# A transformer layer's out and gate products on one core: a fourth place for raw weight pieces

## The chip, the cores and the metric

The kernel runs on one core of one Trainium2 chip. A core has five engines that run side by side, each with its own queue of instructions: TensorE (PE in the profile; its weight loads are listed apart as PEld), VectorE (DVE), ScalarE (ACT), GpSimd (POOL) and SyncE (SP, which here only starts transfers). Transfers between the chip's memory (HBM) and the core's on-chip memory (SBUF) are made by 16 DMA engines. Matrix products land in a second small memory (PSUM), whose banks hold 128 x 512 numbers.

The metric is the device time of one execution in microseconds, the median of several runs. The kernel before takes 797.68 us (three runs, 797.63 to 797.83).

## The reference, cut to what matters

One layer: sliding-window attention over 512 tokens of width 2048, an output product, and a gated embedding. All in float32.

```python
hn = rmsnorm(x, norm_g[0])
y = swa_mixer(hn, ...)               # (attention(hn) * silu(gate)) @ w_out
x = x + y
emb = p[0] @ ple_proj[0]             # 512 x 256 @ 256 x 2048
g = sigmoid(rmsnorm(x, ple_norm[0]) @ ple_gate[0])
x = x + emb * g
return rmsnorm(x, final_g)
```

Two large weighted stages stand behind the attention: the product with `w_out` (2048 x 2048) and the product with `ple_gate` (2048 x 2048).

## The kernel before, in words

**Precision.** TensorE's fast 32-bit format keeps fewer bits than float32. So every operand is split into a high part, rounded to that format, and a low part, the rest; a product is made of three matmuls, high x high, low x high and high x low. The helper `mm3` issues them (lines 128 to 130 of the profile). For a raw weight piece, ScalarE makes the high part (`bhi`, line 675) and VectorE then the low one (`blo`, line 676). This pair is called the split of the piece here.

**Stages.** First the keys, values and first queries; then the remaining projections, with attention woven in (until about 450 us); then the out stage (`w_out`) and the gate stage (`ple_gate`), each computed by Strassen's scheme: seven products of half-size matrices instead of eight, in the order `ORDER_OUT` = 1, 7, 2, 6, 5, 3, 4 and `ORDER_PLE` = 2, 7, 1, 6, 5, 3, 4. The last product of the gate stage ends the kernel, together with the last normalisation and the stores.

**Units and pieces.** A unit is one product p for one half jj of the columns. It takes four pieces of weights of 128 x 1024 numbers (512 KB); each piece serves 12 matmuls of 128 x 512 (two halves, two blocks of tokens, three terms). In the gate stage some units are followed by a piece of `ple_proj` and its 12 matmuls (`e` in the profile; those of the gate are `g`, of the out stage `o`). The pieces of both stages are numbered through, 0 to 111, by the class `Pieces`. Three kinds exist: `one` and `proj` are loaded into a place for raw pieces (tile names `braw`); `seed` and `grow` pieces live in tiles of their own (`grown`), where later weights are added in by GpSimd's transfers.

**Places for raw pieces.** The pool `wpool` has three buffers of the tag `wraw`. `_prepare(n)` takes the next one and has SP start the load (line 668). SP starts the transfers in program order, and each waits until its buffer's previous piece is split. `ahead(i)`, called when TensorE comes to piece i, prepares pieces up to i + 3 and splits up to i + 2; the high and low tiles have three buffers each.

**Sums of the weights and of the left side.** The left operands (`Forms.steps`) are made from the gated attention output (`gate0` to `gate3`): some products need a difference first (VectorE, line 768, 128 x 1024 in place), then the split into `fho` (ScalarE, line 780) and `flo` (VectorE, line 781). Lines 585, 595 and 601 finish the gated output itself.

**What sets the order.** TensorE's and SP's order is the order of the program text everywhere. During the attention all engines' order is written out by hand. From the end of the attention to the first product of the gate stage the order on ScalarE, VectorE and GpSimd is chosen by the framework's scheduler when the program is built, from its own estimate of when operands and buffers come free; from the second product of the gate stage on (`manual_schedule` with all five engines) it is by hand again. Each engine carries out its instructions strictly in that order.

**Pools.** The attention's tiles live in pools that are closed at its end; the pool `late` (in the list `rooms`) takes over their space. A tile of `late` waits for the last user of the bytes under it.

Of the kernel before, what the change touches and what calls it, by code (L numbers as in the profile page):

```python
# [11 lines left out]
F32 = mybir.dt.float32  # L12
# [8 lines left out]
P = 128  # L21
KC = D // P
NB = S // P
# [15 lines left out]
MASKED = -3.0e38  # L39
TOEP = 384  # L40
WARM = 24
PAD = 48
XW = S + 1 + 768


# [11 lines left out]
def trunk_kernel(ctx: ExitStack, tc: tile.TileContext, a: dict):  # L57
    nc = tc.nc

    def pool(name, bufs=1, **kw):  # L60
        return ctx.enter_context(tc.tile_pool(name=name, bufs=bufs, **kw))
# [3 lines left out]
    const = pool("const")  # L65
# [2 lines left out]
    banks_s = ExitStack()  # L68
    others = {"s": banks_s.enter_context(tc.tile_pool(name="psum_s", bufs=2, space=PSUM))}

    const.tile([P, PAD], F32, name="pad")
    pn = const.tile([P, KC], F32, name="pn")

    whole = pool("whole", bufs=4)
    wpool = pool("wpool", bufs=3)
# [12 lines left out]
    WE = 1024  # L88

    class Weights:  # L90


        def __init__(self, ahead):
            self.srcs, self.ahead, self.raw, self.made = [], ahead, [], []

            self.todo, self.asked, self.apart = [], 0, False
# [37 lines left out]
    ident = const.tile([P, P], F32, name="ident")  # L134
    make_identity(nc, ident)

    warm = const.tile([P, 1], F32, name="warm")
    nc.vector.memset(warm, 1.0)
    nc.scalar.activation(warm, warm, AF.Sqrt)
    ones = nc.const_aps.tensor(1.0, [P, P], mybir.dt.bfloat16)  # L140
# [14 lines left out]
    v_ps = [bank(f"vps{t}", "ttoo"[t]) for t in range(NB)]  # L155

    rstd1 = const.tile([P, NB], F32, name="rstd1")
    ssq1 = const.tile([P, NB], F32, name="ssq1")

    def run(gen):  # L160
        for _ in gen:
# [2 lines left out]
    def rsqrt_mean(out, ssq, n, nm):  # L164

        w = out.shape[-1]
        ms = const.tile([P, w], F32, name=f"ms_{nm}")
        rt = const.tile([P, w], F32, name=f"rt_{nm}")
        y = const.tile([P, w], F32, name=f"y_{nm}")
        t = const.tile([P, w], F32, name=f"t_{nm}")  # L170
        nc.vector.tensor_scalar(ms, ssq, 1.0 / n, EPS, op0=ALU.mult, op1=ALU.add)
        nc.scalar.activation(rt, ms, AF.Sqrt)
        yield
        nc.vector.reciprocal(y, rt)
        nc.vector.tensor_mul(t, y, y)
        nc.vector.tensor_mul(t, t, ms)
        nc.vector.tensor_scalar(t, t, -0.5, 1.5, op0=ALU.mult, op1=ALU.add)
        nc.vector.tensor_mul(out, y, t)
# [21 lines left out]
    for k in range(KC):  # L200
# [57 lines left out]
        f, e = k == 0, k == KC - 1  # L258
# [26 lines left out]
        if 3 <= k < 3 + NB:  # L285
            t = k - 3
# [3 lines left out]
        if k == 9:  # L290
            run(rsqrt_mean(rstd1, ssq1, D, "r1"))

            rdram = tc.dram_tile([NB, P], F32, name="rdram")
            nc.gpsimd.dma_start(rdram.rearrange("t p -> p t"), rstd1)
            nc.gpsimd.dma_start(rb, rdram.rearrange("t p -> (t p)").partition_broadcast(P))
# [91 lines left out]
    for b in range(exact, BUCKETS):  # L387
        d = np.nonzero(bk == b)[0]
        if len(d):
            lo, n = P - 1 + int(d.min()), len(d)  # L390
# [229 lines left out]
    rooms = []  # L620
# [7 lines left out]
    def block(nm, r, c, jj, m):  # L628
        return a[nm][2 * (c - 1) + jj, 4 * (r - 1) + m]

    SUMS = [("w_out", 7), ("w_out", 5), ("w_out", 6), ("ple_gate", 7), ("ple_gate", 5)]
    for nm, p in SUMS:
        for jj in range(2):
            for m in range(4):
                t = summed[nm, p, jj, m] = tc.dram_tile([P, WE], F32, name=f"{nm}_{p}_{jj}_{m}")
# [12 lines left out]
    class Pieces:  # L648
# [9 lines left out]
        def _prepare(self, i):  # L658
            kind, src, key = self.specs[i]
            if kind == "grow":  # L660
                t = self.grown[key]
                nc.gpsimd.dma_start(t, src, accum_op=ALU.add)
            else:
                if kind == "seed":
                    t = self.grown[key] = rooms[0].tile([P, WE], F32, tag="grown", name=f"grown{i}", bufs=8)
                else:
                    t = wpool.tile([P, WE], F32, tag="wraw", name=f"braw{i}")
                nc.sync.dma_start(t.rearrange("p (k c) -> p k c", k=2) if kind == "proj" else t, src)
            self.base[i] = t

# [13 lines left out]
            nc.vector.tensor_sub(lo, raw, hi.bitcast(F32))  # L684
            self.made[i] = tuple([t[:, :512], t[:, 512:]] for t in (hi, lo))

        done = 0

        def ahead(self, i):

            last = len(self.specs) - 9
            for n in range(max(i, 0), min(i + 6, last) + 1):
                kind = self.specs[n][0]
                if n not in self.base and n >= self.done and kind != "grow" and (kind == "seed" or n <= i + 3):
                    self._prepare(n)
            while self.done <= min(i + 2, last):
                self._split(self.done)
                self.done += 1
# [298 lines left out]


    rstd2 = const.tile([P, NB], F32, name="rstd2")
    ss2 = const.tile([P, NB], F32, name="ss2")  # L1000
    pT = wpool.tile([P, WE], F32, tag="wraw", name="pT").rearrange("p (k t) -> p k t", k=2)
    nc.sync.dma_start(pT, a["pT"])
    nc.scalar.copy(pTh, pT)
# [1 line left out]
    done = {t: 0 for t in range(NB)}  # L1005
# [81 lines left out]
    for n, p in enumerate(ORDER_PLE[:-1]):  # L1087
# [8 lines left out]
        for jj in range(2):  # L1096
            calls = iter(range(4))

            def todo():
                k = early.get((p, jj, next(calls)))  # L1100
                if turns:
                    turn(*turns.pop(0), "s")
                    if not turns:
                        nc.vector.tensor_reduce(ss2, ssq2, axis=AX.X, op=ALU.add)
                        run(rsqrt_mean(rstd2, ss2, D, "r2"))
                    return
                next(nxt, None)
                if p == 2:
                    next(nxt, None)
                if k is not None:  # L1110
                    split_last(k)

            ps = unit(p, jj, at_ple, ple_forms, todo)
            e = {}
            if p in (1, 5, 3):
                w = B.get(at_ple[p, jj] + 4)
                for t in (0, 1) if p in (1, 3) else (2, 3):
                    e[t] = embed(t, w, "to"[jj])
            if (p, jj) != (3, 1):
                later.insert(0, partial_of(gate_later, p, jj, ps, e))  # L1120
# [5 lines left out]
    w = [B.get(at_ple["e", jj]) for jj in range(2)]  # L1126
    f = ple_forms.made[4]
# [27 lines left out]
    ssum = const.tile([P, 3], F32, name="ssum")  # L1155
    nc.vector.tensor_reduce(ssum[:, :2], ssq3[:, :2, :4], axis=AX.X, op=ALU.add)
    root = rsqrt_mean(yn2[:, :2], ssum[:, :2], D, "r3")
    next(root)
    g = block(0, 0, "s", "o")()
# [30 lines left out]
    next(g)  # L1190
    run(g)

    base, ms, rt, im, ys, nw, yn = (const.tile([P, 1], F32, name=f"{v}_3") for v in ("base", "ms", "rt", "im", "ys", "nw", "yn"))
    g = block(1, 1, "p", "t", slice(0, 256))()
    next(g)
    by_gain(3, 0)
# [2 lines left out]
    n = done[3]  # L1199
# [87 lines left out]
```

## Time and profile before

| what | value |
|---|---|
| median of the runs | 797.68 us |
| the profiled execution | 799.05 us, of which the span (first to last instruction) 797.0 us |
| TensorE busy | 786.0 us, 99% of the span |
| VectorE busy | 589.4 us, 74% |
| ScalarE busy | 500.1 us, 63% |
| mean granted TensorE clock | 0.996 |
| splits of raw pieces, VectorE | 80 of 1.22 us each |
| matmuls 128 x 512 in the two stages | 0.39 us each, overlapped |

How to read the rows in this document: a row of the timeline has start, length, engine, line, operation, result<-operands, shape and count; in square brackets the idle time before it and what ended it. A row merges neighbours ("x2") and its length then covers both. Matmul rows overlap, since the next begins before the last is out of the array; the steps between starts count. In the chain of work that ended last, a row is start, length, engine, result and line. SPq rows are the moments at which SP starts a transfer; how long the transfer takes isn't in their length. A row of a table by stretches gives the stretch, its length, busy time and instructions of PE, PEld, DVE, ACT and POOL, then the granted clock, the DMA engines' share and GB/s.

### The profile page before, as it was taken

The page shows a single profiled execution, that of the slowest core. Times are in us where ns is not written, and L with a number is a line of the kernel's source. Part 1 is how long each engine was busy: PE and PEld are TensorE (multiplying, and loading weights), DVE is VectorE, ACT ScalarE, POOL GpSimd, SP SyncE. Part 2 cuts the span into 40 slices and gives each one's busy share as a digit, 9 for nine tenths or more (in the row PEclk, how much of TensorE's full clock was granted, in tenths as well). Part 3 has the DMA queues.
Part 4 walks back from the last instruction along what each step waited for, and adds up shares of the span by engine and source line. Part 5 has one row for each costly group of instructions (what it writes and reads, how often), then busy time and mean ns, then how long its engine had stood idle before and what let it go on. Part 6 is the DMA issues. An engine that isn't in the chain of part 4 may idle for free.

```text
span 797.0 us, 10975 instructions
## 1 busy us (share of the span) xinstructions
PE 786.0 (99%) x3758; PEld 657.5 (82%) x3758; DVE 589.4 (74%) x1030; ACT 500.1 (63%) x1057; POOL 115.3 (14%) x234
## 2 busy tenths in 40 slices
PE   9999999999999999999999999999999999999995
PEld 8888888888888888888888888888888888878884
DVE  4546697877878597777768898766656656979996
ACT  5742576675766676676756644555568656646855
POOL 0031223131212213131312100020000120200000
PEclk9999999999999999999999999999999999999998
DMA  9882489697878868677865378997503995775533
GB/s 346 282 221 96 119 259 247 164 252 187 221 186 241 225 180 230 191 234 162 260 161 145 120 276 308 371 248 242 190 28 127 360 219 192 157 204 196 183 106 106
DMA packets 42343, 164.23 MB, mean 206 GB/s; under 512 B 5984, under 2 KB 7008, under 8 KB 38448
## 3 DMA queue, kind: packets, MB, share of 16 engines
q1 hardware_dynamic: 35456, 129.67, 47.7%
q0 software_dynamic: 6832, 33.88, 23.0%
q8 instruction: 29, 0.48, 0.3%
q14 instruction: 26, 0.21, 0.1%
HBM read 157.70 MB, written 46.19 MB: 256 GB/s over the span
## 4 chain that ended last, share of the span: by engine, by line
PE 95%; DVE 2%; DMA 1%; ACT 0%; issue 0%; ACTq 0%; DVEq 0%
PE gps L128 7%; PE gps L130 7%; PE gps L129 7%; PE qps L128 7%; PE qps L130 7%; PE qps L129 7%; PE o L128 6%; PE o L130 6%; PE o L129 6%; PE g L129 5%; PE g L130 4%; PE g L128 4%; PE s L463 2%; PE o L558 2%; PE vps L280 2%; PE pt L516 2%
## 5 line engine op out<-in xcount | busy, mean ns | idle before, releaser
L676 DVE TENSOR_TENSOR blo<-braw,bhi 128x1024 fp32r<-128x1024 f32 x80 | 97.5, 1221 | 40.3 <-ACT bhi L675 40.1
L675 ACT CAST bhi<-braw 128x1024 fp32r<-128x1024 f32 x80 | 84.0, 1051 | 64.9 <-PE o L130 22.7
L128 PE MATMUL gps<-xh,whi 128*128 128x512 f32 x256 | 99.9, 390 | 0.1
L130 PE MATMUL gps<-xh,wlo 128*128 128x512 f32 x256 | 99.8, 390 | 0.0
L129 PE MATMUL gps<-xl,whi 128*128 128x512 f32 x256 | 99.8, 390 | 0.0
L128 PE MATMUL o<-bhi,fho 128*128 128x512 f32 x224 | 87.7, 391 | 0.0
L128 PE MATMUL qps<-xh,whi 128*128 128x512 f32 x224 | 87.7, 391 | 0.0
L130 PE MATMUL qps<-xh,wlo 128*128 128x512 f32 x224 | 87.4, 390 | 0.0
L129 PE MATMUL qps<-xl,whi 128*128 128x512 f32 x224 | 87.3, 390 | 0.0
L129 PE MATMUL o<-blo,fho 128*128 128x512 f32 x224 | 87.2, 389 | 0.0
L130 PE MATMUL o<-bhi,flo 128*128 128x512 f32 x224 | 87.2, 389 | 0.0
L129 PE MATMUL g<-blo,fhg 128*128 128x512 f32 x192 | 75.1, 391 | 0.6 <-DVE blo L676 0.6
L128 PE MATMUL g<-bhi,fhg 128*128 128x512 f32 x192 | 75.1, 391 | 0.0
L112 DVE TENSOR_TENSOR wlo<-wraw,whi 128x1024 fp32r<-128x1024 f32 x60 | 73.8, 1231 | 1.7 <-ACT whi L111 1.3
L130 PE MATMUL g<-bhi,flg 128*128 128x512 f32 x192 | 74.8, 390 | 0.0
L532 POOL TENSOR_SCALAR_AFFINE_SELECT own<-r 64x512 fp32r<-64x512 f32 (+1 forms) x48 | 32.4, 675 | 254.8 <-DVE r L522 254.8
L521 ACT CAST r<-pt 128x256 fp32r<-128x256 f32 x64 | 23.8, 371 | 71.8 <-PE pt L516 71.5
L522 DVE TENSOR_TENSOR r<-pt,r 128x256 fp32r<-128x256 f32 x64 | 27.1, 423 | 55.7 <-ACT r L521 54.9
L111 ACT CAST whi<-wraw 128x1024 fp32r<-128x1024 f32 x60 | 62.3, 1040 | 4.4 <-issue 3.9
L676 DVE TENSOR_TENSOR blo<-grown,bhi 128x1024 fp32r<-128x1024 f32 x32 | 39.1, 1223 | 23.6 <-ACT bhi L675 21.9
L130 PEld LDWEIGHTS gps<-xh,wlo 128*128 128x128 f32 x256 | 48.1, 188 | 10.1
L128 PEld LDWEIGHTS gps<-xh,whi 128*128 128x128 f32 x256 | 48.1, 188 | 9.4 <-PE vps L280 0.5
(206 smaller groups left out, 1738.8 us busy)
## 6 DMA issues: line engine op xcount, KB each, us to landing
wraw<-in_w_gate_in SPq DMA_DIRECT2D x32, 512.0 KB, 5.9
wraw<-in_w_q SPq DMA_DIRECT2D x28, 512.0 KB, 5.0
w_out<-in_w_out POOLq DMA_DIRECT2D x24, 512.0 KB, 7.7
braw<-in_w_out SPq DMA_DIRECT2D x24, 512.0 KB, 4.3
braw<-in_ple_gate SPq DMA_DIRECT2D x24, 512.0 KB, 4.5
xw<-in_first SPq DMA_DIRECT2D x14, 640.5 KB, 6.6
w_out<-in_w_out SPq DMA_DIRECT2D x16, 512.0 KB, 6.2
ple_gate<-in_ple_gate SPq DMA_DIRECT2D x16, 512.0 KB, 6.6
```

What stands on the lines that cost most here:

```text
L111: nc.scalar.copy(hi, raw)
L112: nc.vector.tensor_sub(lo, raw, hi.bitcast(F32))
L128: nc.tensor.matmul(ps, sh, mh, start=first, stop=False, skip_group_check=more)
L129: nc.tensor.matmul(ps, sh, ml, start=False, stop=False, skip_group_check=more)
L130: nc.tensor.matmul(ps, sl, mh, start=False, stop=last, skip_group_check=more)
L280: nc.tensor.matmul(v_ps[t], h[:, c], both[:, :, 256:512], start=f, stop=e, skip_group_check=True)
L463: nc.tensor.matmul(s_ps[:, u, : 2 * n], st, key[:, :, first : first + n], start=True, stop=True)
L521: nc.scalar.copy(rh, src)
L522: nc.vector.tensor_sub(rl, src, rh.bitcast(F32))
L532: nc.gpsimd.affine_select(out=flat(own), in_=flat(r).bitcast(F32), pattern=[[0, 8], [sign, HB]], compare_op=ALU.is_ge, fill=0.0, base=-HB ...
L675: nc.scalar.copy(hi, raw)
L676: nc.vector.tensor_sub(lo, raw, hi.bitcast(F32))
```

## The change

In the two weighted stages a fourth place for raw pieces is added: a tile of the tag `fourth` in the pool `late`. Every fourth raw piece goes there; the others go round the three old buffers. Pieces are asked for four ahead instead of three (once `late` exists, so from piece 3 on). `late` has to be 4096 bytes per partition larger. Room is made among the small tiles: a pad of 48 numbers is dropped, the work columns of the reciprocal roots (`ms`, `rt`, `y`, `t`) share tags, and so do `ssq1` with `ss2` and `warm` with `im_3`.

```diff
-    const.tile([P, PAD], F32, name="pad")
-    warm = const.tile([P, 1], F32, name="warm")
+    warm = const.tile([P, 1], F32, tag="one", name="warm")
-    ssq1 = const.tile([P, NB], F32, name="ssq1")
+    ssq1 = const.tile([P, NB], F32, tag="sums", name="ssq1")
...
     def rsqrt_mean(out, ssq, n, nm):
         w = out.shape[-1]
-        ms = const.tile([P, w], F32, name=f"ms_{nm}")
-        rt = const.tile([P, w], F32, name=f"rt_{nm}")
-        y = const.tile([P, w], F32, name=f"y_{nm}")
-        t = const.tile([P, w], F32, name=f"t_{nm}")
+        of = nm if w == 1 else "r"
+        ms, rt, y, t = (
+            const.tile([P, 1 if w == 1 else NB], F32, tag=f"{v}_{of}", name=f"{v}_{nm}")[:, :w]
+            for v in ("ms", "rt", "y", "t")
+        )
...
     def _prepare(self, i):
...
-                    t = wpool.tile([P, WE], F32, tag="wraw", name=f"braw{i}")
+                    self.raws += 1
+                    if rooms and self.raws % 4 == 0:
+                        t = rooms[0].tile([P, WE], F32, tag="fourth", name=f"braw{i}")
+                    else:
+                        t = wpool.tile([P, WE], F32, tag="wraw", name=f"braw{i}")
...
-        done = 0
+        done = raws = 0
...
     def ahead(self, i):
...
-                if n not in self.base and n >= self.done and kind != "grow" and (kind == "seed" or n <= i + 3):
+                if n not in self.base and n >= self.done and kind != "grow" and (kind == "seed" or n <= i + (4 if rooms else 3)):
                     self._prepare(n)
...
-    ss2 = const.tile([P, NB], F32, name="ss2")
+    ss2 = const.tile([P, NB], F32, tag="sums", name="ss2")
...
-    base, ms, rt, im, ys, nw, yn = (const.tile([P, 1], F32, name=f"{v}_3") for v in ("base", "ms", "rt", "im", "ys", "nw", "yn"))
+    base, ms, rt, ys, nw, yn = (const.tile([P, 1], F32, name=f"{v}_3") for v in ("base", "ms", "rt", "ys", "nw", "yn"))
+    im = const.tile([P, 1], F32, tag="one", name="im_3")
```

The built programs have the same instructions on every engine. The order is the same on TensorE, ScalarE and GpSimd. It differs on SP by the loads that are asked for a piece earlier, and on VectorE in two stretches of the out stage, around pieces 3 to 8 and around pieces 17 and 18. Lines of the changed kernel are numbered four higher than before in the two stages.

More of the change, by code (lines that the diff above doesn't have):

```diff
@@ L41 @@
 WARM = 24
-PAD = 48
 XW = S + 1 + 768
```

## The prediction

> **What bounds the kernel.** I read the page's busy times first, then the chain that ended last, then TensorE's rows wherever that chain leaves TensorE. TensorE (PE) is busy 99% of the span and carries 95% of the chain, so only its gaps are worth anything.
>
> ```profile
> span 797.0 us, 10975 instructions
> PE 786.0 (99%) x3758; PEld 657.5 (82%) x3758; DVE 589.4 (74%) x1030; ACT 500.1 (63%) x1057; POOL 115.3 (14%) x234
> PE 95%; DVE 2%; DMA 1%; ACT 0%; issue 0%; ACTq 0%; DVEq 0%
> ```
>
> In the two weighted stages the chain leaves PE at one place before the tail, through a transfer (start, length):
>
> ```profile
> 700.38 1.23 DVE blo L676
> 701.62 9.11 DMA braw<-ple_gate
> 710.83 1.06 ACT bhi L675
> 711.91 1.24 DVE blo L676
> 713.20 0.50 PE g L129
> 746.13 0.48 PE g L129
> 749.12 0.36 PE g L129
> ```
>
> That is piece 93. All three places were full until the split of piece 90 ended at 701.62; its load then took 9.11 us. TensorE's own rows price this and the two later entries:
>
> ```profile
> 712.19 0.39 PE L128 MATMUL g<-bhi,fhg 128*128 128x512 f32 x1
> 713.20 0.50 PE L129 MATMUL g<-blo,fhg 128*128 128x512 f32 x1 [0.61 <-DVE blo L676]
> 715.82 0.39 PE L128 MATMUL e<-bhi,pTh 128*128 128x512 f32 x1
> 743.02 0.39 PE L128 MATMUL e<-bhi,pTh 128*128 128x512 f32 x1
> 751.61 0.39 PE L128 MATMUL g<-bhi,fhg 128*128 128x512 f32 x1
> ```
>
> Matmuls of this shape start 0.2267 us apart: 715.82 to 743.02 is 27.20 us for 120 of them (ten pieces of twelve: two halves, two token blocks, three products). From 712.19 to 715.82 are 12 starts, due 2.72 us, taken 3.63: **0.91 us lost**. Of this 0.78 is the gap (713.20 against 712.42) and 0.13 a slow restart. From 743.02 to 751.61 are 36 starts, due 8.16, taken 8.59: **0.43 lost**. So the stages have 1.34 us of stall.
>
> **The change, part by part.** *Shared columns, the pad removed.* No instruction is added or removed on any engine; a shared column's earlier readers are done long before it is written again. Zero. Without that cover one such write would wait for one reader, an instruction of this length, in the tail:
>
> ```profile
> 789.43 0.16 DVE L1213 RECIPROCAL im<-ms 128x1 f32<-128x1 f32 x1
> ```
>
> *A fourth place.* Before, the load of piece n waits for the split of n-3, now for that of n-4. Pieces 93 and 103 show what this moves, with the issues of the transfers and the casts:
>
> ```profile
> 678.09 0.32 SPq L668 DMA_DIRECT2D braw<-ple_gate  x1
> 701.62 0.32 SPq L668 DMA_DIRECT2D braw<-ple_gate  x1
> 726.57 0.33 SPq L668 DMA_DIRECT2D braw<-in_ple_gate  x1
> 731.49 0.33 SPq L668 DMA_DIRECT2D braw<-in_ple_gate  x1
> 736.66 1.05 ACT L675 CAST bhi<-braw 128x1024 fp32r<-128x1024 f32 x1 [2.70 <-DVE flg L781]
> 737.74 1.23 DVE L676 TENSOR_TENSOR blo<-braw,bhi 128x1024 fp32r<-128x1024 f32 x1 [1.08 <-ACT bhi L675]
> ```
>
> Piece 92 was issued at 678.09, its place just free; 93 can follow it within some 4 us instead of at 701.62, and 94 takes the slot of 701.62. Even with the same 9.11 us, 94 lands at 710.73 and is split by 713.0, and TensorE first wants it at 715.82 (the e row). So 0.91 goes; next late is nothing nearer than 2.8 us. Piece 103 was issued at 731.49 and cast only at 736.66, 5.17 later; the flg the row names cannot release a cast of weights, so I read a landing. The issue moves to the slot of 726.57, the cast no longer waits, and VectorE (DVE) gets back the 1.08 us it stood idle, more than 105 and 106 were late by. So 0.43 goes too. Gain 1.34 us. Bytes and transfers are unchanged.
>
> *The first use of the fourth place.* Its bytes lie under the last pair's queries, so the first load (piece 3) waits for TensorE's last scores:
>
> ```profile
> 437.85 5.54 SPq L668 DMA_DIRECT2D braw<-in_w_out  x2
> L463 PE MATMUL s<-k,q x4: 312/312/313, 428.7 to 434.5; 128*128 128x320 f32 x4
> ```
>
> These end at 434.8, before piece 2 is issued at 437.85; piece 3, the second of that row (443.07), moves up to 438. Behind it on SP stand only later pieces. Zero.
>
> *What the scheduler does with it.* DVE's order in the out stage is not written out by hand, and the built order differs. TensorE's, ScalarE's and GpSimd's do not. DVE, after the last gate values:
>
> ```
> before: blo3, flo7_10, blo4, flo7_11, gate0-=, blo5, gate1-=, gate0-=, blo6
> after:  flo7_10, flo7_11, gate0-=, gate1-=, gate0-=, blo3, gate1-=, blo4, blo5, blo6
> ```
>
> Five instructions (two of L781, three of L768) now stand ahead of the low half of piece 3, which TensorE needs soon. DVE's rows there before, with the ScalarE (ACT) casts and TensorE's rows that they meet:
>
> ```profile
> 456.60 1.28 DVE L585 SCALAR_TENSOR_TENSOR gate<-gate,u 128x512 f32<-128x512 f32 x2
> 457.80 1.22 DVE L676 TENSOR_TENSOR blo<-braw,bhi 128x1024 fp32r<-128x1024 f32 x1
> 458.94 0.68 DVE L781 TENSOR_TENSOR flo<-gate,fho 128x512 fp32r<-128x512 f32 x1
> 459.54 1.22 DVE L676 TENSOR_TENSOR blo<-braw,bhi 128x1024 fp32r<-128x1024 f32 x1
> 461.27 1.22 DVE L768 TENSOR_TENSOR gate<-gate,gate 128x1024 f32<-128x1024 f32 x1
> 462.41 1.22 DVE L676 TENSOR_TENSOR blo<-braw,bhi 128x1024 fp32r<-128x1024 f32 x1
> 455.17 0.62 ACT L780 CAST fho<-gate 128x512 fp32r<-128x512 f32 x1
> 455.69 1.05 ACT L675 CAST bhi<-braw 128x1024 fp32r<-128x1024 f32 x1
> 451.90 0.40 PE L128 MATMUL o<-bhi,fho 128*128 128x512 f32 x1
> 460.31 0.39 PE L129 MATMUL o<-blo,fho 128*128 128x512 f32 x1
> 497.31 1.22 DVE L676 TENSOR_TENSOR blo<-braw,bhi 128x1024 fp32r<-128x1024 f32 x1
> 450.00:460.00 10.00, 10.00 (x47) 8.34 (x46) 9.96 (x14) 6.99 (x11) 0.04 (x1) 1.00 0.31 107
> ```
>
> DVE is full there (9.96 of 10 us, the windows row), so nothing hides in a hole. All inputs of the five are ready: their last cast ends at 455.79, the gate values before 457.9. Back to back, an L781 takes a step of 0.60 (458.94 to 459.54) and an L768 1.14 (461.27 to 462.41). So blo3 starts at 457.80 + 2 x 0.60 + 3 x 1.14 = 462.42 and ends 1.22 later, at 463.64. Before, it ended at 459.02, 1.29 us ahead of the matmul at 460.31 (the 38th of the stage). That matmul now starts 0.05 after 463.64, as at 713.20 after 713.15: at 463.69, **3.38 us late**, and with the slow restart 0.13 the loss is 3.51. Taking full lengths rather than steps (0.68 and 1.22) gives 463.64 + 0.40 and 3.91: the upper end; the lower, if DVE's start were as much as 0.3 earlier through earlier landings, 3.2.
>
> It ends there: blo4 follows after one more L768 at 464.68 and ends at 465.90, and TensorE reaches it 2.72 after 463.82, at 466.54; blo5 is steps ahead of its need. TensorE is the bound, so nothing gives the time back; what follows is released by TensorE and shifts with it. The order differs once more, where three adds (0.6 each) pass ahead of piece 18: it was split at 497.31 and is due at 451.90 + 18 x 2.72 + 0.23 = 501.09, so 1.8 us do not reach it.
>
> **Sum:** 3.51 - 0.91 - 0.43 = +2.17 us. The profiled execution took 799.05 us (span 797.0 and 2.05 around it), the median of the runs is 797.68; the stalls are the same kind of steps in both, so I add the sum to the median: **799.85 us**, +0.27%. About 0.2% (1.6 us) is what a measurement of this kernel can tell from no change.
>
> **Weighed against a rule.** The granted clock at the end of the span (last column but two):
>
> ```profile
> 786.00:788.00 2.00, 1.52 (x13) 1.32 (x12) 1.79 (x8) 0.68 (x2) 0.00 (x0) 1.00 0.02 8
> 788.00:790.00 2.00, 0.00 (x0) 0.00 (x0) 1.71 (x8) 1.71 (x3) 0.00 (x0) 1.00 0.00 0
> 790.00:792.00 2.00, 0.00 (x0) 0.00 (x0) 1.51 (x4) 1.41 (x3) 0.00 (x0) 0.56 0.20 76
> ```
>
> TensorE stops at 787.52; the clock is whole to 790 and 0.56 on average to 792, so it halves near 790.24, 2.7 us later. The new gap, from the end of the matmul a step before 460.31 (460.08 and 0.39) to 463.69, is 3.2 us. The gap of 0.61 us at 713 halved nothing. The Trainium skill, TensorE: Matmul & The Clock Gate, "Part 1", says the clock halves after an idle window of about 3.4 us, windows running free of the kernel; by it 3.2 us of idle fill no window, and my sum would stand; the trace, which halves after 2.7, does not quite agree.
>
> **Rivals.** (1) *The clock halves in the new gap.* For: 3.2 is over 2.7. Against: at the end the idle followed a nearly empty piece, and it depends on where the gap falls. If it falls about when TensorE resumes, it costs half of the time until it is granted again; 2.7 us as the one delay that I have gives 1.35: 801.2; twice that, 802.5. (2) *Faster: no stall at 460.* It ends on the other side if blo3 is done by 460.26, that is, if the five (4.62 us of steps) fit in holes of DVE before 457.80; then 797.68 - 1.34 = 796.34. The 9.96 of 10 speaks against. (3) *It does not do what it says:* early loads collide with the adds in memory, landing grows with the number under way, and both stalls stay: 797.68 + 3.51 = 801.2. Against: bytes do not grow. (4) *Part-way:* the five overlap better and the stall is 2.9 or less: within 0.2%.
>
> **How the numbers follow.** The sum as it stands 0.56, the clock 0.24, the loads 0.06, part-way 0.08, faster 0.06. The likeliest gives 799.85, with its own range 799.4 to 800.4. For 8 in 10 I reach up to the clock's 801.6 and down to 799.2. Slower by over 0.2%: 0.86; within: 0.08; faster: 0.06.
>
> **What would show it.** In the profile after: a gap of 3.2 us before a matmul on blo near 460.4, released by DVE's blo; ahead of it three L768 (there under a later line) in a row; all DMA issues of the stage one piece earlier; no gap near 716 and 749; the granted clock 1.00 from 460 to 470. I am wrong if blo3 is split before 460, if a new gap stands where the waits of SP were, or if the clock falls in that stretch.

## The result and the profile after

| | before | after |
|---|---|---|
| median of five runs | 797.73 us (797.63 to 798.29) | 803.04 us (802.47 to 803.70) |
| the profiled execution | 799.05 us, span 797.0 | 803.04 us, span 801.0 |

The changed kernel is slower: the ratio is 1.0063, with a 95% interval of 1.0052 to 1.0075. That is 5.31 us between the medians, where +2.17 was forecast; 803.04 lies above the range. The profiled execution of after happens to be its median; that of before is 1.37 us above its own (799.05 against 797.68 of the forecast), which will matter below.

TensorE's rows around 460 us, from the timeline of the kernel after (start, length, engine, line, operation; in brackets the idle time before and what ended it):

```profile
460.36 0.39 PE L128 MATMUL o<-bhi,flo 128*128 128x512 f32 x1
460.59 0.39 PE L126 MATMUL o<-bhi,fho 128*128 128x512 f32 x1
464.19 0.67 PE L127 MATMUL o<-blo,fho 128*128 128x512 f32 x1 [3.22 <-DVE blo L680]
464.66 0.63 PE L128 MATMUL o<-bhi,flo 128*128 128x512 f32 x1
465.08 0.63 PE L126 MATMUL o<-bhi,fho 128*128 128x512 f32 x1
467.22 0.63 PE L128 MATMUL o<-bhi,flo 128*128 128x512 f32 x1
467.64 0.46 PE L126 MATMUL o<-bhi,fho 128*128 128x512 f32 x1
467.94 0.40 PE L127 MATMUL o<-blo,fho 128*128 128x512 f32 x1
468.18 0.39 PE L128 MATMUL o<-bhi,flo 128*128 128x512 f32 x1
```

The step from 460.59 is 3.60 us where 0.2267 is due: 3.37 us late. Then, instead of 0.23, the steps are 0.43 (464.66 to 465.08) until 467.64. From 460.59 to 467.94 are ten steps, due 2.27, taken 7.35: 5.08 us lost in one place. VectorE's rows there:

```profile
456.50 0.69 DVE L594 SCALAR_TENSOR_TENSOR gate<-gps,gate 128x512 f32<-128x512 f32 x1
457.11 1.28 DVE L584 SCALAR_TENSOR_TENSOR gate<-gate,u 128x512 f32<-128x512 f32 x2
458.31 1.29 DVE L785 TENSOR_TENSOR flo<-gate,fho 128x512 fp32r<-128x512 f32 x2
459.51 3.49 DVE L772 TENSOR_TENSOR gate<-gate,gate 128x1024 f32<-128x1024 f32 x3
462.92 1.22 DVE L680 TENSOR_TENSOR blo<-braw,bhi 128x1024 fp32r<-128x1024 f32 x1
```

Two L785 and three L772 stand ahead of the low half of piece 3 (L680 at 462.92, done at 464.14). Its cast was done long before, and its load as well:

```profile
456.20 1.04 ACT L679 CAST bhi<-braw 128x1024 fp32r<-128x1024 f32 x1
```

So VectorE had the operands at 457.24 and was merely ordered to do something else first. What the stall did to the clock is in the table by stretches (stretch, its length, busy time and instructions of PE, PEld, DVE, ACT, POOL, granted clock, DMA share, GB/s). The stretches are cut where the trace's clock records change, at 464.36 and 467.78, and the same length earlier and later:

```profile
457.54:460.95 3.41, 3.41 (x16) 2.50 (x14) 3.41 (x6) 1.22 (x2) 0.00 (x0) 1.00 0.21 84
460.95:464.36 3.41, 0.19 (x2) 0.17 (x2) 3.41 (x4) 0.88 (x1) 0.00 (x0) 1.00 0.00 0
464.36:467.78 3.42, 3.42 (x9) 2.68 (x10) 3.18 (x3) 0.00 (x0) 0.00 (x0) 0.50 0.52 180
467.78:471.19 3.41, 3.41 (x17) 2.79 (x16) 1.23 (x1) 1.12 (x2) 0.00 (x0) 1.00 0.91 280
```

After a stretch in which TensorE was busy 0.19 us, it runs at half clock for exactly one stretch. What that costs follows from the rows: from 464.66 to 467.64 are seven steps, 2.98 us where 1.59 is due, and at that rate a whole stretch of 3.41 us loses 1.6 (less than half of it, since the step at whole clock, 0.227 us, is more than half of the 0.426 at half clock). 3.37 and 1.6 are 4.97; the 0.11 left of 5.08 is about the slow restart that the prediction put at 0.13.

Later in the two stages nothing is left of the waits of before. TensorE's waits of the whole execution, and two stretches that answer to the places of the old stalls, which lie some 4 us later here:

```profile
PE o L127 <- DVE blo L680: 3.2, 1, 3.2
710.00:718.00 8.00, 8.00 (x37) 6.64 (x36) 6.87 (x8) 4.16 (x5) 0.00 (x0) 1.00 0.92 290
745.00:754.00 9.00, 9.00 (x41) 7.46 (x40) 8.93 (x11) 7.44 (x11) 0.00 (x0) 1.00 0.53 150
```

Between the two traces, counted by TensorE's starts, the offset is +0.50 already at 460.36 (the start-up, which differs from execution to execution), 5.59 behind the slow stretch, then 0.89 less at 713 and 0.43 less at 749. So against that one execution the gain is there. Between the medians of five runs it does not show: 5.08 of the 5.31 is the place at 460. But 41 later runs of before, beside the experiments below, have a median of 798.31; 803.04 is 4.73 above that, and then a gain of some 0.35 us would stand against the 5.08.

### The profile page after: what moved, and what is told of

The parts are those of the page before. It is cut to its first block, busy times and chain, and to the rows that moved or that the text cites. A ratio compares the mean times of both kernels' runs of the same rounds, so it can differ in the third digit from the quotient of the medians.

```text
span 801.0 us, 10978 instructions
## 1 busy us (share of the span) xinstructions
PE 786.9 (98%) x3758; PEld 658.6 (82%) x3758; DVE 590.5 (74%) x1030; ACT 500.3 (62%) x1057; POOL 111.9 (14%) x234
## 4 chain that ended last, share of the span: by engine, by line
PE 95%; DVE 2%; ACT 1%; issue 0%; DMA 0%; ACTq 0%; DVEq 0%
PE qps L126 7%; PE qps L128 7%; PE qps L127 7%; PE gps L126 7%; PE gps L128 7%; PE gps L127 7%; PE o L127 6%; PE o L128 6%; PE o L126 6%; PE g L128 5%; PE g L127 5%; PE g L126 5%; PE s L462 2%; PE vps L279 2%; PE o L557 2%; PE pt L515 2%
## 5 line engine op out<-in xcount | busy, mean ns | idle before, releaser
L680 DVE TENSOR_TENSOR blo<-braw,bhi 128x1024 fp32r<-128x1024 f32 x80 | 97.5, 1222 | 41.0 <-ACT bhi L679 40.9
L680 DVE TENSOR_TENSOR blo<-grown,bhi 128x1024 fp32r<-128x1024 f32 x32 | 39.1, 1223 | 23.6 <-ACT bhi L679 23.2
```

## The experiments

Each kernel was timed in alternation with the kernel before, in two sets; a ratio is against the runs of before in its own set (median 798.36 us in the first, 798.29 in the second, which holds the kernel with four matmuls, the columns alone and the repeat of the fourth place).

**The kernel before, once more** (no edit). Are the stalls at 713 and 746 part of every execution?

> The kernel before once more, for a second profiled execution of it. Theory A (the two stalls of 0.91 and 0.43 us belong to the one execution that was profiled, 799.05 us, and not to the usual one): 797.7 us, and a profiled execution of about 797.7 shows no gap of TensorE near 712 and 746. Theory B (the stalls are in every execution): 797.7 us with both gaps in the profile, and the change's gain of 1.34 us is inside its 803.04.

Eleven runs: 798.13 us (797.56 to 798.89), ratio 0.9999 [0.9991, 1.0008]. Its profiled execution took 797.77 us, span 795.8. By stretches:

```profile
708.00:716.00 8.00, 8.00 (x37) 6.64 (x36) 6.92 (x8) 5.83 (x7) 0.00 (x0) 1.00 0.60 208
743.00:752.00 9.00, 9.00 (x42) 7.44 (x41) 8.08 (x8) 8.29 (x10) 0.00 (x0) 1.00 0.59 183
```

The same stretches in the trace of before that the prediction shows:

```profile
708.00:716.00 8.00, 7.39 (x33) 5.81 (x32) 4.96 (x6) 4.94 (x6) 0.00 (x0) 1.00 0.43 160
743.00:752.00 9.00, 9.00 (x39) 6.94 (x38) 8.96 (x10) 8.33 (x13) 0.00 (x0) 1.00 0.48 163
```

In the new trace TensorE makes 37 and 42 matmuls there where the first made 33 and 39: the stalls are gone. Piece 93 was asked for at the same time, and came sooner:

```profile
701.74 0.32 SPq L668 DMA_DIRECT2D braw<-ple_gate  x1
708.83 1.05 ACT L675 CAST bhi<-braw 128x1024 fp32r<-128x1024 f32 x1 [3.44 <-DMA braw<-ple_gate]
```

The cast waits for the transfer and starts 7.09 us after the issue; in the first trace it was 9.21 (701.62 to 710.83). So three places were enough here, and the stall of the first trace came from a late landing. Of the 1.34 us of gain in my sum nothing was there to be won in this execution.

**One late piece alone.** Three places and three pieces ahead as before; only the fourth raw piece (piece 3) goes to the tile in `late`. VectorE's order around it is that of after, SP's that of before.

```diff
-                    if rooms and self.raws % 4 == 0:
+                    if self.raws == 4:
...
-... n <= i + (4 if rooms else 3)):
+... n <= i + 3):
```

> The changed kernel with three places and pieces asked for three ahead as before; only piece 3 still lies in the pool late, which keeps VectorE's changed order around pieces 3 to 8. Theory A (the whole loss is VectorE's order: 3.38 us of stall and one stretch of 3.41 us at half the granted clock, 1.70): 802.8 us. Rival (the fourth place itself costs, by its earlier transfers): 797.7 us.

Five runs: 803.50 us (801.27 to 804.49), ratio 1.0063 [1.0050, 1.0076]. The place at 460, timeline and stretches:

```profile
460.60 0.39 PE L126 MATMUL o<-bhi,fho 128*128 128x512 f32 x1
464.20 0.80 PE L127 MATMUL o<-blo,fho 128*128 128x512 f32 x1 [3.21 <-DVE blo L680]
460.42:463.83 3.41, 0.57 (x3) 0.14 (x1) 3.41 (x4) 1.04 (x1) 0.00 (x0) 1.00 0.00 0
463.83:467.24 3.41, 3.04 (x7) 2.48 (x8) 3.41 (x4) 0.00 (x0) 0.00 (x0) 0.50 0.00 0
```

The same stall, the same half clock, the whole loss, without a fourth place and without earlier loads. One of the five runs, 801.27, is 2.2 us below the median of the five and had a mean clock of 0.996, against 0.992 to 0.995 of the others. I read it as an execution in which the clock did not halve; it was not traced.

**The fourth place without that piece.** Four ahead as in after, but the fourth place is used from the eighth raw piece on, and piece 3 goes round the old three. VectorE's order around piece 3 is that of before.

```diff
-                    if rooms and self.raws % 4 == 0:
+                    if self.raws > 4 and self.raws % 4 == 0:
```

> The changed kernel with the fourth place used from the eighth raw piece on instead of the fourth; pieces are asked for four ahead throughout. VectorE's order around pieces 3 to 8 is then that of the kernel before. Theory A: no stall near 460, the granted clock 1.00 throughout; 796.4 us if the stalls near 712 and 746 are in usual executions of the kernel before, 797.6 if they are not. Rival (the fourth place itself costs): 801 us or more.

Eleven runs: 797.81 us (797.39 to 798.23), ratio 0.9993 [0.9984, 1.0002]. Eleven more beside another set of the kernel before:

> The same kernel as fourth_from8, for a second comparison. Theory A (the place removes stalls that only some executions of the kernel before have): 0.3 to 0.6 us below the kernel before and a narrower spread, with no run near the upper end of before's. Rival (it does nothing): the same median and the same spread as the kernel before.

798.08 us (797.34 to 798.34), ratio 0.9995 [0.9986, 1.0004]. VectorE and TensorE in the traced execution of this second set:

```profile
459.64 0.69 DVE L785 TENSOR_TENSOR flo<-gate,fho 128x512 fp32r<-128x512 f32 x1
460.25 1.22 DVE L680 TENSOR_TENSOR blo<-braw,bhi 128x1024 fp32r<-128x1024 f32 x1
460.00:464.00 4.00, 4.00 (x20) 3.30 (x19) 4.00 (x5) 1.35 (x2) 0.00 (x0) 1.00 0.82 296
464.00:468.00 4.00, 4.00 (x19) 3.34 (x18) 4.00 (x5) 2.35 (x3) 0.00 (x0) 1.00 0.87 306
```

A split stands between the steps again, TensorE has no hole, the clock is whole. So the fourth place itself does no harm. What it gains is 0.55 and 0.21 us, and each interval by itself holds 1: at most some 1.3 us (0.9984). Taken together, the 22 runs have a median of 797.86 and the 41 runs of before beside them 798.31, and 19 of these 41 lie above 798.34, the slowest of the 22. So a gain of some 0.45 us, a third of the 1.34 in my sum, is likely. That it comes from late landings being caught would fit, but is not shown.

**The stall with TensorE kept busy.** Nine matmuls of 128 x 512 on constants stand between the first and the second matmul of the place where TensorE waits for piece 3. Their result is not used; they only fill the wait.

```diff
+                    if (forms.nm, p, jj, k, tb) == ("o", 1, 0, 6, 0):
+                        nc.tensor.matmul(ps[tb], fh[:, kk, blk(tb)], bh[kk], start=False, stop=False, skip_group_check=True)
+                        fill_ps = bank("fill_ps", "p")
+                        for _ in range(9):
+                            nc.tensor.matmul(fill_ps, ones, row_of_ones, start=True, stop=True)
...
```

> The changed kernel with nine matmuls of constants (128x512, into a bank that is overwritten later; their result is not used) put into TensorE's queue where it waits for the low half of piece 3: about 2 of the 3.2 us of idle are filled, the waiting is not shortened. Theory A (1.70 us of the loss are the halved clock after the idle): the clock stays 1.00, 801.3 us. Rival (the clock has no part in it, the loss is waiting alone): 803.0 us.

Five runs: 801.20 us (800.76 to 801.55), ratio 1.0037 [1.0023, 1.0051]. Timeline, then stretches cut by this execution's clock records:

```profile
460.30 0.39 PE L915 MATMUL o<-bhi,fho 128*128 128x512 f32 x1
460.76 1.91 PE L918 MATMUL fill_ps<-const-bfloat16-1.0 128*128 128x512 bf16 x8
463.89 0.50 PE L919 MATMUL o<-blo,fho 128*128 128x512 f32 x1 [1.22 <-DVE blo L680]
464.23 0.40 PE L920 MATMUL o<-bhi,flo 128*128 128x512 f32 x1
464.47 0.40 PE L126 MATMUL o<-bhi,fho 128*128 128x512 f32 x1
466.56 0.39 PE L126 MATMUL o<-bhi,fho 128*128 128x512 f32 x1
462.84:466.25 3.41, 2.36 (x10) 1.95 (x11) 3.41 (x4) 0.00 (x0) 0.00 (x0) 1.00 0.39 129
```

TensorE resumes just as late, 463.89 after 460.30, but the steps are short from the third matmul on, and the clock stays whole. From 460.30 to 466.56 are twelve steps of the product, due 2.72 us, taken 6.26: 3.54 lost, 1.54 less than the 5.08 above. The median, 801.20, is 1.84 under 803.04, which was timed in an earlier set; the kernel with one late piece, timed in the same set but without a fourth place, took 2.30 more. I take the clock's share from the traces, 1.5 to 1.6 us; the medians agree in kind. The rest is the late split's.

**The same with four matmuls** instead of nine (`range(4)`), so that TensorE idles for 2.3 us.

> As fill9 with four matmuls of constants instead of nine: some 0.9 of the 3.2 us of idle are filled, 2.3 us stay. If the clock is judged over stretches of 3.41 us that fall at random and a stretch that is 20% busy is still taken for idle (as the one at the end of the span is), a stretch around this gap is at best 31% busy: the clock stays whole if the limit lies below that, and the time is 801.3 us as with nine; if 31% still counts as idle, some executions halve and others don't, 801 to 803 us with a spread of over 1 us.

Five runs: 801.43 us (800.90 to 802.47), ratio 1.0041 [1.0026, 1.0055]. They fall into two groups: 802.47 and 802.39 with a mean clock of 0.995, and 800.90, 801.29 and 801.43 with 0.997. The traced one is 802.47:

```profile
463.64 0.50 PE L919 MATMUL o<-blo,fho 128*128 128x512 f32 x1 [2.33 <-DVE blo L680]
461.67:465.08 3.41, 1.44 (x6) 1.22 (x7) 3.41 (x4) 0.00 (x0) 0.00 (x0) 1.00 0.14 31
465.08:468.49 3.41, 3.41 (x9) 2.64 (x9) 1.92 (x2) 0.94 (x1) 0.00 (x0) 0.50 0.79 274
```

Here 1.44 us of work in a stretch was not enough. The other group is read from times and mean clocks alone. With the same kernel and the same idle time it depends on the execution whether the clock halves, which is what cuts at a different time in each execution would do.

**The shared columns alone.** No fourth place, three ahead, columns and pad as in after.

```diff
-                    if rooms and self.raws % 4 == 0:
+                    if False:
...
-... n <= i + (4 if rooms else 3)):
+... n <= i + 3):
```

> The shared columns and the dropped pad alone: three places, three ahead, all engines' order that of the kernel before. Every theory: within 0.2% of the kernel before, 798.3 us; a loss or a gain here would have to be taken out of the other differences.

Eleven runs: 798.49 us, ratio 1.0005 [0.9996, 1.0014]. Nothing, as forecast. With its three places this kernel is also a third look at the old stalls. TensorE does not wait at 713, and at the second place it loses 0.23 us: the rows below are 48 steps apart, due 10.88, taken 11.11.

```profile
745.38 0.39 PE L126 MATMUL g<-bhi,fhg 128*128 128x512 f32 x1
756.49 0.39 PE L126 MATMUL e<-bhi,pTh 128*128 128x512 f32 x1
```

## Why the prediction was wrong, point by point

**The late split: right.** Forecast were a gap of 3.2 us and a matmul 3.38 late; the rows have 3.22 and 3.37. VectorE was full and stays full, nothing is given back later, piece 4 and the adds at piece 18 make no second stall. Counting the five steps from the built order and the rows of before was enough. The piece alone brings it (803.50), and without that piece it is gone (797.81, 798.08).

**The first use of the fourth place and the columns: right.** Piece 3 was cast at 456.20 with no wait for a transfer, and the columns alone changed nothing.

**The gain of 0.91 and 0.43: the first step that failed.** Both stalls do go, against the execution shown. But I had taken them from one execution of 799.05 us and subtracted them from a median of 797.68, on the ground that "the stalls are the same kind of steps in both". They were not in both: before's second traced execution lacks them, and is about as much faster (797.77 against 799.05) as they were long (1.34); the kernel with the columns alone has only 0.23 of them. What a fourth place saves in the usual run is more like the 0.45 us between the 22 runs and the 41. The 1.37 us between execution and median, which stands in my own text, was the sign. Set against its own execution, the sum gives 799.05 + 2.17 = 801.2; set against the median, it had to be made without the gain, 797.68 + 3.38 + 0.13 = 801.2 again. That is the time of a stall at whole clock, and the kernel with the filled wait has a median of 801.20. So close a match is in part luck: the kernel before took 798.36 beside it, which leaves 2.84 and not 3.5 for the filled wait; between the traced executions it is 801.12 against 797.77, or 3.35.

**The clock: the second step that failed.** The likeliest case had it whole from 460 to 470; it halved for 3.41 us. Rival (1) had the mechanism, with a chance of 0.24 that was too small and a price of 1.35 us that measured 1.6. I took the price from the 2.7 us between TensorE's end and the halving; but that is the distance from the end to a boundary of the stretches, which says nothing of their length. The weight followed from asking whether 3.2 us of idle time is long enough. The rows show that the question is how busy TensorE is within a stretch. At the end of the span in the trace of before, where I read the 2.7:

```profile
786.84:790.25 3.41, 0.69 (x6) 0.48 (x5) 2.97 (x13) 2.42 (x5) 0.00 (x0) 1.00 0.00 0
790.25:793.66 3.41, 0.00 (x0) 0.00 (x0) 1.36 (x3) 1.37 (x3) 0.00 (x0) 0.50 0.56 199
711.75:715.16 3.41, 2.80 (x13) 2.00 (x12) 3.25 (x4) 3.41 (x6) 0.00 (x0) 1.00 0.30 107
```

0.69 us of work in the stretch before, and it halved; 2.80 at the old stall, and it did not. The ends of two other traces, the kernel with four matmuls (two rows) and the second set of the fourth place without piece 3 (two rows), cut by their own clock records:

```profile
789.34:792.76 3.42, 1.94 (x17) 1.74 (x15) 2.50 (x10) 1.68 (x2) 0.00 (x0) 1.00 0.00 0
792.76:796.17 3.41, 0.00 (x0) 0.00 (x0) 2.29 (x9) 2.12 (x6) 0.00 (x0) 1.00 0.24 91
784.85:788.27 3.42, 2.04 (x18) 1.84 (x16) 2.50 (x10) 1.58 (x2) 0.00 (x0) 1.00 0.00 0
788.27:791.68 3.41, 0.00 (x0) 0.00 (x0) 2.39 (x9) 2.21 (x6) 0.00 (x0) 1.00 0.21 76
```

With the experiments: 0.19, 0.57, 0.69 and 1.44 us of 3.41 halved the next stretch; 1.94, 2.04, 2.36 and 2.80 did not. (In these stretches nearly all of the idle time lies in one piece, so the rows cannot tell the share of work in a stretch from the length of the idle piece in it.) A gap of 3.2 us leaves one stretch with at most 1.8 us of work wherever the cuts fall. If they fall at random, I estimate from these numbers that nearly eight executions in ten have a stretch with 1.44 or less. So halving was the likely case and not a rival. The Trainium skill, TensorE: Matmul & The Clock Gate, "Part 1", gives windows of about 3.4 us that run free of the kernel; the rows agree, with 3.41 and with boundaries at another place in each execution. Its wording that the clock falls after an idle window I had read as a window without any work, and that the rows contradict.

The two steps that failed, 1.34 and 1.6 us, are 2.9 of the 3.19 us by which 803.04 lies above 799.85; the rest is less than the spread of the five runs (802.47 to 803.70).

**The other rivals.** Loads that collide (3): the stage with the earlier loads and the old order on VectorE is not slower (0.9993 and 0.9995), so it falls. Faster with no stall (2) and part-way (4) fall with the row at 464.19.

**What stays open.** Why the scheduler puts five instructions ahead of the split is not visible in a trace. Piece 3 lies over a tile of the attention that is read until late, and the one-piece kernel shows that its place alone moves the order; that the scheduler's estimate took it as ready later than it is, is argued only. Where between 1.44 and 1.94 us of work the clock's decision lies is not known. That the changed kernel gains 0.35 to 0.45 us from its fourth place in the usual run is likely, but no interval here shows it. The traced spans differ by 0.3 us less than TensorE's offsets (4.0 against 4.27, the sum of +0.50, +5.08 and the two gains); that lies behind TensorE's last stall, and I did not follow it.

## What to carry to other kernels

Read a stall that is to be removed in a second execution, or at least hold the profiled execution's own time against the median: what exceeds it is not there to be won. When a tile moves to another pool, compare the built order on every engine, since an in-order engine that is full makes a stall of each instruction put ahead of an urgent one. And price a long stall of TensorE with the half clock that can follow it: here 1.6 us on 3.37, after 3.2 us of idle in most executions and after 2.3 us in some.

## What the hardware showed beside that

The granted clock changed only at whole multiples of 3.41 us within an execution: in the trace of after its records run 3.56 to 464.36 whole, to 467.78 half, to 795.46 whole (135, 1 and 96 stretches). The first boundary lay between 3.56 and 6.61 us after the start in the nine traces. That would explain why the same idle time of 2.3 us gave about 802.4 in some executions of one kernel and about 801.2 in others; only one of these was traced.

Half clock shows in a row as a step of 0.43 us instead of 0.23 for 128 x 512, with a length of 0.63 instead of 0.39. And nine matmuls without use made the kernel faster than leaving TensorE idle: by 1.54 us in the traces, by 1.84 between the medians.
